# Two early product groups at each norm, a last norm without POOL, and a start with zero products: one decoder layer in fp32 on one core

## The chip, the core and the metric

The kernel runs on one core of a Trainium2 chip. The core has a matmul engine (PE, with a separate weight load, PEld), a vector engine (DVE), a scalar engine (ACT), a general engine (POOL) and an engine that issues the transfers (SP). Each runs its own instructions in order and waits on semaphores for the others. The metric is the device time of one execution in microseconds (us), as the median of several runs.

## The reference

One inference step of a decoder layer on 320 token columns: 256 of a new sequence and 8 x 8 of running ones. Weights and activations are fp32.

```python
x1 = layer_norm(ALPHA * x + 0.5 * swiglu_ffn(x, ffn1_w1, ffn1_w3, ffn1_w2), ln1_g, ln1_b)
proj = x1 @ w_in
q, k, v, o, ig, fg, glu_a, glu_b, gate_a, gate_b = jnp.split(proj, SPLIT_IDX, axis=-1)
h_a, (C_new, n_new, m_new) = mlstm_branch(q, k, v, o, ig, fg, ...)
h_b, conv_new = conv_branch(glu_a, glu_b, conv_buf, conv_w, conv_b, conv_ln_g, conv_ln_b)
mix = (sigmoid(gate_a) * h_a + sigmoid(gate_b) * h_b) @ w_out
x2 = layer_norm(ALPHA * x1 + mix, ln2_g, ln2_b)
y = layer_norm(ALPHA * x2 + 0.5 * swiglu_ffn(x2, ffn2_w1, ffn2_w3, ffn2_w2), ln3_g, ln3_b)
```

D_MODEL is 2048, D_FF 5632, there are four mLSTM heads, and the depthwise convolution has 31 taps. The results are y for both groups, the new mLSTM states and the new convolution caches.

## The kernel before

Activations lie transposed: 16 tiles of 128 features x 320 tokens. A product of a weight column (128 output features) is a sum over 16 tiles, one 128x128 weight block each. For fp32 accuracy each weight block and each activation tile is split into a high and a low part: ACT copies the high part (`whi`, L148; `xh`), DVE subtracts to get the low part (`wlo`, L149; `xl`). `mm3` issues three products per block: `xh`*`whi` (L213), `xl`*`whi` (L214), `xh`*`wlo` (L215).

`Stream` brings the weights in the order of use, in chunks of 512 KB (8 blocks), and splits them half a chunk at a time, three halves ahead. Accumulators are PSUM tiles: five named `acc`, three named `sm`.

The stages follow each other: FFN1, norm ln1, the mixer (products with w_in, the heads, the convolutions, the convolution's norm), the products with w_out, norm ln2, FFN2, the last norm ln3, output yT.

A norm needs the sums over all 16 tiles before its factor `r` is known (`Norm.finish`, then `rsqrt`, L239 to L243). Then each tile is scaled (`z`, L1094), and split with its bias (`affine_split`: `xh` on ACT at L500, `xl` on DVE at L501). So that PE has work in that time, `Norm.early` holds tiles `eh`, `el` of the tile that is centred but not yet scaled (`ahead`), with two columns more for the gain and the bias. `first_group` multiplies a first group of four weight columns with them; `normed` (L287 to L291, tile `late`) puts the factor and the offset into these results afterwards. At ln1 the group is the first two pairs of convolution inputs (`a`, `g`), at ln2 two pairs of FFN2's up-products.

Smaller work runs beside the products. `gemm` calls `tick` every four blocks, and a tick takes one step of each of four lanes: heads and gates in lane 0, norm steps in lane 1, two convolutions in lanes 2 and 3. `w_in_schedule` sets the order of the 112 columns of w_in: `a`/`g` pairs of the convolutions, one at each step, with the other columns spread over the steps; a head starts when its last `v` column is done (`head`, whose first product is `pb`, L674), and 16 `gb` columns and the last head's `o`/`ga` columns come at the end. In that end part the convolution's norm (`conv_out`, `th` at L248) and the last head's own norm (`mean` at L270 and `sq`) run.

The tile framework's scheduler decides from its own plan in which order each engine's instructions stand; `issue_after` keeps an instruction behind another one. All transfers are issued by SP and go through one queue.

Of the kernel before, what the change touches and what calls it, by code (L numbers as in the profile page):

```python
# [9 lines left out]
F32 = mybir.dt.float32  # L10
F32R = mybir.dt.float32r
AF = mybir.ActivationFunctionType
ALU = mybir.AluOpType
# [31 lines left out]
def w_in_schedule():  # L45


    def qkv(h):
        return ([("q", 2 * h + j) for j in range(2)] + [("k", 2 * h + j) for j in range(2)]
                + [("v", 4 * h + j) for j in range(4)])  # L50

    def oga(h):
        return [x for j in range(4) for x in (("o", 4 * h + j), ("ga", 4 * h + j))]

    others = qkv(0) + qkv(1) + oga(0) + qkv(2) + oga(1) + qkv(3) + oga(2)
    groups = [[("a", 0), ("g", 0), ("a", 1), ("g", 1)]]
    steps = range(2, KD)
    done = 0
    for n, i in enumerate(steps):
        groups += [[("a", i)], [("g", i)]]  # L60
        upto = len(others) * (n + 1) // len(steps)
        groups += [[x] for x in others[done:upto]]
        done = upto
    tail = [("gb", j) for j in range(KD)] + oga(3)
    return groups + [[x] for x in tail]
# [105 lines left out]
class Kernel:  # L171
    TICK = 4

# [43 lines left out]
    def gemm(self, accs, xs):  # L217

        n = len(xs)
        for k, (xh, xl) in enumerate(xs):  # L220
# [73 lines left out]
    def first_group(self, count, norm, name):  # L294

        accs = [self.acc(T + 2) for _ in range(count)]
        ys = []

        def tiles():
            for k in range(KD):  # L300
                ys.append(self.affine_split(*norm.scaled(k, name)))
                norm.z[k] = None
                yield

        self.later(tiles(), 1)
        self.gemm(accs, norm.early)
        self.drain((1,), lambda: len(ys) == KD)
        norm.early.clear()
        return [self.normed(ps, norm) for ps in accs], ys
# [9 lines left out]
    def build(self):  # L319
        tc, nc, a = self.tc, self.nc, self.a  # L320
        with (
# [10 lines left out]
            def x(n):  # L332
                k = len(xs)
                n = min(n, KD - k)
                raw = mp.tile([P, n * T], F32, tag="c0", name="xraw", bufs=3)
                nc.sync.dma_start(out=raw, in_=a["xT"][:, k * T:(k + n) * T])
                xs.extend(self.split(raw[:, i * T:(i + 1) * T]) for i in range(n))

            x(1)
# [81 lines left out]
    def ffn(self, n, xs, norm=None):  # L421
# [5 lines left out]
        for kind, q, ms in ffn_schedule():  # L427
            if kind == "up":
                if xs is None:
                    accs, xs = self.first_group(2 * len(ms), norm, "ln2")  # L430
# [28 lines left out]
    def last_norm(self, norm):  # L459

        nc = self.nc
        by_pe, by_pool = (0, 4, 8, 12), (3, 7, 11, 15)
        z, d = norm.z, {}

        def centre(k):
            eng = nc.gpsimd if k in by_pool else nc.vector
            eng.tensor_tensor(out=z[k], in0=z[k], in1=norm.mean, op=ALU.subtract)
            d[k] = z[k]

        with self.tc.issue_after(norm.sums.ins):  # L470
            for k in by_pe:
# [3 lines left out]
        for k in (3, 7, 1):  # L475
            centre(k)
        with self.tc.issue_after(norm.var.ins):
            for k in (2, 5, 6, 9, 11, 15):
                centre(k)
        first = None  # L480
        for k in list(d) + [k for k in range(KD) if k not in d]:
            with self.tc.issue_after((norm.last if k in d else first).ins):
                if k not in d:
                    centre(k)
                eng = nc.gpsimd if k in by_pool else nc.vector
                mul = eng.tensor_tensor(out=z[k], in0=d[k], in1=norm.r, op=ALU.mult)  # L486
                if eng is nc.vector and first is None:
                    first = mul
                g, b = self.scol("ln3_g", -0.5, k), self.col("ln3_b", k)
                if k % 3 == 1:  # L490
                    nc.vector.tensor_scalar(z[k], z[k], g, b, op0=ALU.mult, op1=ALU.add)
                else:
                    nc.scalar.activation(z[k], z[k], AF.Identity, scale=g, bias=b)
                nc.sync.dma_start(out=self.a["yT"][k], in_=z[k])
# [109 lines left out]
    def conv(self, i, acc_a, acc_g, done):  # L604
# [5 lines left out]
        nc.sync.dma_start(out=us[:, :, :HIST], in_=a["cache"][i])  # L610
# [273 lines left out]
    def mixer(self, before):  # L884
# [32 lines left out]
        self.silu_done = 0  # L917
        for n, group in enumerate(w_in_schedule()):
            if ys is None:
                accs, ys = self.first_group(len(group), before, "ln1")  # L920
# [35 lines left out]
            if n == 2:  # L956
                self.gates_product(ys)
# [221 lines left out]
```

## Time and profile before

| | |
|---|---|
| median of 3 runs | 2965.38 us (2963.70 to 2968.78) |
| profiled execution | 2962.41 us, its span 2960.6 us |
| instructions on PE | 19582 |
| mean granted PE clock | 0.993 |
| weights and other data read | 433.12 MB |

The span runs from the first to the last instruction of the profiled execution. Busy time is the time in which an engine worked; a busy PE can still be a slow one, since the granted clock may be half. A chunk of 8 blocks has 24 products. Line numbers in rows are those of the kernel before; in rows of the changed kernel the same lines stand a little lower (L213 becomes L214, L501 becomes L520).

### The profile page before, as it was taken

What the parts mean: (1) busy time and instruction counts of PE and PEld (TensorE: products, weight loads), DVE (VectorE), ACT (ScalarE), POOL (GpSimd) and SP (SyncE); (2) the same over time, 40 slices, a digit from 0 to 9 for tenths busy, and PEclk for the clock granted to TensorE, in tenths of its full rate; (3) what the DMA queues carried; (4) which work ended last, traced back from release to release, by engine and by line L of the source; (5) the groups of instructions that cost most, each with busy time, mean ns of one, the idle gap of its engine ahead of it and who ended that gap; (6) DMA issues with size and microseconds to landing.
All of it is one profiled execution on the core that took longest, in us unless ns stands there. A gap on an engine that the chain in (4) does not pass through costs nothing.

```text
span 2960.6 us, 50364 instructions
## 1 busy us (share of the span) xinstructions
PE 2900.5 (98%) x19582; PEld 2867.5 (97%) x19582; DVE 1892.2 (64%) x3491; ACT 1346.7 (45%) x2396; POOL 70.6 (2%) x76
## 2 busy tenths in 40 slices
PE   9999999999999899999999989999999999999997
PEld 9999999999999899999999979999999999999997
DVE  6544444444458999989989886578544444444447
ACT  5433433433445555555554555455433433433444
POOL 0100000000000000000000000200100000000001
PEclk9999999999999999999999999999999999999999
DMA  6444444444444456564565634444444444444443
GB/s 217 152 150 151 150 150 150 150 150 150 150 150 142 122 150 206 170 210 149 178 197 160 215 103 157 150 150 136 150 150 150 150 150 150 150 150 150 150 150 106
DMA packets 163264, 460.14 MB, mean 155 GB/s; under 512 B 50220, under 2 KB 53164, under 8 KB 163024
## 3 DMA queue, kind: packets, MB, share of 16 engines
q1 hardware_dynamic: 163024, 456.92, 47.4%
q8 instruction: 153, 2.51, 0.4%
q14 instruction: 87, 0.71, 0.1%
HBM read 433.12 MB, written 23.74 MB: 154 GB/s over the span
## 4 chain that ended last, share of the span: by engine, by line
PE 93%; DMA 2%; DVE 2%; ACT 1%; issue 0%; DVEq 0%; SPq 0%; ACTq 0%
PE acc L213 30%; PE acc L214 30%; PE acc L215 30%; DMA c<-in_C 1%; DMA out_C_s<-c 1%; PE ip L820 1%; DVE wlo L149 0%; PE cps L826 0%; PE sp L689 0%; ACT whi L148 0%; PE num L847 0%; DMA xraw<-in_xT 0%; DVE z L1094 0%; DVE z L486 0%; DVE c L827 0%
## 5 line engine op out<-in xcount | busy, mean ns | idle before, releaser
L149 DVE TENSOR_TENSOR wlo<-wraw,whi 128x512 fp32r<-128x512 f32 x1568 | 1086.7, 695 | 909.7 <-ACT whi L148 902.0
L148 ACT ACTIVATE whi<-wraw 128x512 fp32r<-128x512 f32 x1568 | 986.6, 631 | 1393.0 <-PE acc L214 1282.5
L213 PE MATMUL acc<-xh,whi 128*128 128x320 f32 x4480 | 1386.4, 311 | 24.0 <-ACT th L248 7.6
L214 PE MATMUL acc<-xl,whi 128*128 128x320 f32 x4480 | 1383.8, 309 | 6.9 <-DVE xl L501 6.9
L215 PE MATMUL acc<-xh,wlo 128*128 128x320 f32 x4480 | 1384.9, 310 | 0.7 <-DVE wlo L149 0.7
L213 PEld LDWEIGHTS acc<-xh,whi 128*128 128x128 f32 x4480 | 843.8, 189 | 31.8 <-ACT th L248 8.5
L214 PEld LDWEIGHTS acc<-xl,whi 128*128 128x128 f32 x4480 | 845.1, 189 | 12.1 <-DVE xl L501 8.0
L215 PEld LDWEIGHTS acc<-xh,wlo 128*128 128x128 f32 x4480 | 843.3, 188 | 5.7 <-DVE wlo L149 0.9
L214 PE MATMUL acc<-hl,whi 128*128 128x320 f32 x1408 | 433.9, 309 | 0.0
L213 PE MATMUL acc<-hh,whi 128*128 128x320 f32 x1408 | 432.9, 308 | 0.3 <-ACT whi L148 0.3
L215 PE MATMUL acc<-hh,wlo 128*128 128x320 f32 x1408 | 432.4, 309 | 0.0
L213 PEld LDWEIGHTS acc<-hh,whi 128*128 128x128 f32 x1408 | 264.3, 188 | 0.6 <-ACT whi L148 0.6
L214 PEld LDWEIGHTS acc<-hl,whi 128*128 128x128 f32 x1408 | 264.1, 188 | 0.0
L215 PEld LDWEIGHTS acc<-hh,wlo 128*128 128x128 f32 x1408 | 264.0, 188 | 0.0
L622 DVE SCALAR_TENSOR_TENSOR cy<-pu,cw,cy 128x256 f32<-128x256 f32 x480 | 222.6, 482 | 1.0
L448 DVE SCALAR_TENSOR_TENSOR z<-acc,z 128x320 f32<-128x320 f32 x128 | 62.8, 491 | 53.9 <-PE acc L215 52.3
L214 PE MATMUL acc<-ml,whi 128*128 128x320 f32 x256 | 79.1, 309 | 0.0
L213 PE MATMUL acc<-mh,whi 128*128 128x320 f32 x256 | 79.1, 309 | 0.0
L215 PE MATMUL acc<-mh,wlo 128*128 128x320 f32 x256 | 78.7, 309 | 0.0
L438 DVE TENSOR_TENSOR h<-s,acc 128x320 f32<-128x320 f32 x86 | 42.0, 488 | 53.3 <-ACT s L436 53.2
L315 POOL TENSOR_TENSOR z<-xh,xl 128x320 f32<-128x320 f32 x48 | 60.6, 1271 | 619.5 <-DVE h L438 353.6
L436 ACT ACTIVATE s<-acc 128x320 f32<-128x320 f32 x86 | 37.7, 438 | 70.2 <-PE acc L215 70.2
(289 smaller groups left out, 1661.9 us busy)
## 6 DMA issues: line engine op xcount, KB each, us to landing
wraw<-in_wst SPq DMA_DIRECT2D x783, 512.0 KB, 3.3
c<-in_C SPq DMA_DIRECT2D x32, 512.0 KB, 4.3
out_C_s<-c SPq DMA_DIRECT2D x32, 512.0 KB, 4.4
out_yT<-z SPq DMA_DIRECT2D x16, 160.0 KB, 1.8
out_C_p<-cn SPq DMA_DIRECT2D x4, 512.0 KB, 2.6
us<-in_cache SPq DMA_DIRECT2D x16, 120.0 KB, 4.5
out_conv_s<-us SPq DMA_DIRECT2D x16, 120.0 KB, 6.2
xraw<-in_xT SPq DMA_DIRECT2D x3, 480.0 KB, 4.4
```

Of the source, the lines that this page charges most:

```text
L148: nc.scalar.activation(hi, raw, AF.Copy)
L149: nc.vector.tensor_tensor(out=lo, in0=raw, in1=hi.bitcast(F32), op=ALU.subtract)
L213: mm(ps, hi, xh, start=first, stop=False)
L214: mm(ps, hi, xl, start=False, stop=False)
L215: mm(ps, lo, xh, start=False, stop=last)
L315: self.nc.gpsimd.tensor_tensor(out=t, in0=hi.bitcast(F32), in1=lo.bitcast(F32), op=ALU.add)
L436: nc.scalar.activation(s, accs[2 * j], AF.Silu)
L438: nc.vector.tensor_tensor(out=hh, in0=s, in1=accs[2 * j + 1], op=ALU.mult)
L448: nc.vector.scalar_tensor_tensor(out=z[m], in0=ps, scalar=0.5 / ALPHA, in1=z[m], op0=ALU.mult, op1=ALU.add)
L622: nc.vector.scalar_tensor_tensor(out=yp, in0=pu[:, w:w + SEQ], scalar=self.cw[:, i, w:w + 1], in1=yp, op0=ALU.mult, op1=ALU.add)
L820: mm(ip[:32, :], qc[j][:, bs], x, start=j == 0 and n == 0, stop=j == 1 and n == 1)
```

## The change

1. `first_group` becomes `first_groups`, a generator: the first group of four columns as before, then a second group of two columns (one `acc` and one `sm` accumulator) from the same early tiles, which are let go one by one (`clear`). The scaling steps are spread over more ticks. At ln1 the third `a`/`g` pair is moved into the second group; `steps` then has 13 entries instead of 14, over which the other 56 columns are spread. At ln2 the second group is FFN2's third pair. The gates' product is called after the second group.
2. `warm_up` sets a tile to zero and multiplies it 13 times by itself, ahead of all weights.
3. `consts` (and the first cache loads of the convolutions) are issued behind the last load of x.
4. `last_norm`: nine tiles instead of four are centred by PE (identity times tile, minus the mean), the other seven by DVE, none by POOL; all 16 gains and biases are applied by ACT, and the tiles go out in the order of their numbers.

```diff
-    groups = [[("a", 0), ("g", 0), ("a", 1), ("g", 1)]]
-    steps = range(2, KD)
+    groups = [[("a", 0), ("g", 0), ("a", 1), ("g", 1)], [("a", 2), ("g", 2)]]
+    steps = range(3, KD)
...
-    def first_group(self, count, norm, name):
-
-        accs = [self.acc(T + 2) for _ in range(count)]
+    def first_groups(self, norm, name):
+
         ys = []
 
         def tiles():
+            yield
+            yield
             for k in range(KD):
                 ys.append(self.affine_split(*norm.scaled(k, name)))
                 norm.z[k] = None
                 yield
-
+                if k % 3 == 2:
+                    yield
+
+        accs = [self.acc(T + 2) for _ in range(4)]
         self.later(tiles(), 1)
         self.gemm(accs, norm.early)
+        yield [self.normed(ps, norm) for ps in accs]
+        del accs
+        accs = [self.acc(T + 2), self.sm([P, T + 2], "acc")]
+        self.gemm(accs, norm.early, True)
         self.drain((1,), lambda: len(ys) == KD)
         norm.early.clear()
-        return [self.normed(ps, norm) for ps in accs], ys
+        yield [self.normed(ps, norm) for ps in accs]
+        yield ys
...
+            self.warm_up()
             x(1)
             for _ in st.load(CB // PB):
                 x(1)
...
-            self.consts(cp)
-            norm = self.ffn(1, xs)
+            norm = self.ffn(1, xs, cp=cp)
...
+    def warm_up(self):
+
+        x = self.t("zero", F32R)
+        self.nc.vector.memset(x.bitcast(F32), 0.0)
+        ps = self.sm([P, T], "zero")
+        for i in range(self.WARM):
+            self.nc.tensor.matmul(ps, x[:, :P], x, start=i == 0, stop=i == self.WARM - 1)
...
+            if i == 3 and cp:
+                with self.tc.issue_after(self.last_x):
+                    self.consts(cp)
...
-        by_pe, by_pool = (0, 4, 8, 12), (3, 7, 11, 15)
+        by_pe = (0, 1, 2, 4, 6, 8, 10, 12, 14)
+        by_dve = [k for k in range(KD) if k not in by_pe]
...
-        with self.tc.issue_after(norm.sums.ins):
-            for k in by_pe:
+        with self.tc.issue_after(norm.var.ins):
+            for k in by_dve[:3]:
+                centre(k)
+        prev = norm.last
+        for k in range(KD):
+            if k in by_pe:
                 d[k] = self.acc()
                 nc.tensor.matmul(d[k], self.ident, z[k], start=True, stop=False)
                 nc.tensor.matmul(d[k], self.minus_mean, norm.s, start=False, stop=True)
...
+            with self.tc.issue_after(prev.ins):
                 if k not in d:
                     centre(k)
...
+                prev = nc.vector.tensor_tensor(out=z[k], in0=d[k], in1=norm.r, op=ALU.mult)
+            nc.scalar.activation(z[k], z[k], AF.Identity, scale=self.scol("ln3_g", -0.5, k), bias=self.col("ln3_b", k))
+            nc.sync.dma_start(out=self.a["yT"][k], in_=z[k])
...
-            if n == 2:
+            if n == 1:
                 self.gates_product(ys)
```

What that does to the order shows at three places. A row is a line of the kernel, the operation and its tiles; x3 means three in a row.

SP at the start of the program, before: the constants `cst`, `btri`, `par` and `cw` stand between the loads of x.

```order
L136 DMA wraw<-in_wst 128x1024 x3
L356 DMA cst<-in_cst 128x360
L364 DMA btri<-in_cst 64x64
L336 DMA xraw<-in_xT 128x640
L368 DMA par<-in_par 128x160
L370 DMA cw<-in_cw 128x496
L336 DMA xraw<-in_xT 128x640
```

The same place in the changed kernel.

```order
L136 DMA wraw<-in_wst 128x1024 x3
L349 DMA xraw<-in_xT 128x640 x2
L136 DMA wraw<-in_wst 128x1024
L349 DMA xraw<-in_xT 128x960
L136 DMA wraw<-in_wst 128x1024 x3
L349 DMA xraw<-in_xT 128x960 x2
L377 DMA cst<-in_cst 128x360
```

The x loads have moved ahead of the constants, and directly behind the third chunk of weights.

DVE at ln1, before, from the norm's factor `r` on: all scaling (`z`) first, then all `xl`, then `late`, then the first convolution (`pu`, `us`).

```order
L243 SCALAR_TENSOR_TENSOR r<-rsq,r 128x320
L1088 TENSOR_TENSOR mr<-mean,r 128x320
L1094 SCALAR_TENSOR_TENSOR z<-z,ln_g_scaled,r 128x320 x15
L501 SCALAR_TENSOR_TENSOR xl<-z,par,xh 128x320
L1094 SCALAR_TENSOR_TENSOR z<-z,ln_g_scaled,r 128x320
L501 SCALAR_TENSOR_TENSOR xl<-z,par,xh 128x320 x15
L289 TENSOR_TENSOR late<-acc,r 128x320 x4
```

The same engine in the changed kernel, a later piece of the same stage, behind the first eleven `xl` and all `late` (`taps` and the reduction into `cy` are a convolution's sample tokens, `cy<-pu,cw,cy` is one tap).

```order
L663 TENSOR_REDUCE cy<-taps 128x32
L149 TENSOR_TENSOR wlo<-wraw,whi 128x512
L642 SCALAR_TENSOR_TENSOR cy<-pu,cw,cy 128x256
L633 TENSOR_TENSOR pu<-th,late 128x256
L634 TENSOR_TENSOR us<-th,late 128x8x8
L149 TENSOR_TENSOR wlo<-wraw,whi 128x512
L642 SCALAR_TENSOR_TENSOR cy<-pu,cw,cy 128x256
L661 TENSOR_TENSOR taps<-us,cw 128x992
L642 SCALAR_TENSOR_TENSOR cy<-pu,cw,cy 128x256
L520 SCALAR_TENSOR_TENSOR xl<-z,par,xh 128x320
```

The last row is the twelfth `xl`: the starts of two convolutions (`pu`, `us`, `taps`) and seven of their taps have moved ahead of or between the last five `xl`, and weight splits `wlo` stand among them.

PE at the last norm, before: the two sums, then the centring of four tiles (`cst` holds the identity).

```order
L1078 MATMUL ps<-ns,mean_d 128x320
L1079 MATMUL pq<-sq,mean_d 128x320
L473 MATMUL acc<-z,cst 128x320
L474 MATMUL acc<-ns,minus_mean 128x320
L473 MATMUL acc<-z,cst 128x320
```

PE at the last norm in the changed kernel.

```order
L506 MATMUL acc<-z,cst 128x320 x5
L1101 MATMUL ps<-ns,mean_d 128x320
L507 MATMUL acc<-ns,minus_mean 128x320 x5
L1102 MATMUL pq<-sq,mean_d 128x320
L506 MATMUL acc<-z,cst 128x320
L507 MATMUL acc<-ns,minus_mean 128x320
```

Five identity products have moved ahead of the first sum and five mean products ahead of the second.

More of the change, by code (lines that the diff above doesn't have):

```diff
@@ L172 @@
     TICK = 4
+    WARM = 13
     def __init__(self, tc, a):
@@ L215, in mm3, with gemm @@
         mm(ps, lo, xh, start=False, stop=last)
-    def gemm(self, accs, xs):
+    def gemm(self, accs, xs, clear=False):
         n = len(xs)
-        for k, (xh, xl) in enumerate(xs):
+        for k in range(n):
+            xh, xl = xs[k]
+            if clear:
+                xs[k] = None
             for ps in accs:
@@ L335, in x @@
                 raw = mp.tile([P, n * T], F32, tag="c0", name="xraw", bufs=3)
-                nc.sync.dma_start(out=raw, in_=a["xT"][:, k * T:(k + n) * T])
+                self.last_x = nc.sync.dma_start(out=raw, in_=a["xT"][:, k * T:(k + n) * T]).ins
                 xs.extend(self.split(raw[:, i * T:(i + 1) * T]) for i in range(n))
+            self.warm_up()
             x(1)
@@ L419, in consts, with ffn @@
             self.kst.append(t)
-    def ffn(self, n, xs, norm=None):
+    def ffn(self, n, xs, norm=None, cp=None):
         nc = self.nc
@@ L426, in ffn @@
         new = Norm(self, z, EPS / ALPHA ** 2, "ln1" if n == 1 else None, KD)
-        for kind, q, ms in ffn_schedule():
+        first = None if xs else self.first_groups(norm, "ln2")
+        for i, (kind, q, ms) in enumerate(ffn_schedule()):
+            if i == 3 and cp:
+                with self.tc.issue_after(self.last_x):
+                    self.consts(cp)
             if kind == "up":
-                if xs is None:
-                    accs, xs = self.first_group(2 * len(ms), norm, "ln2")
+                if first and i < 2:
+                    accs = next(first)
+                    if i == 1:
+                        xs = next(first)
                 else:
@@ L461, in last_norm @@
         nc = self.nc
-        by_pe, by_pool = (0, 4, 8, 12), (3, 7, 11, 15)
+        by_pe = (0, 1, 2, 4, 6, 8, 10, 12, 14)
+        by_dve = [k for k in range(KD) if k not in by_pe]
         z, d = norm.z, {}
         def centre(k):
-            eng = nc.gpsimd if k in by_pool else nc.vector
-            eng.tensor_tensor(out=z[k], in0=z[k], in1=norm.mean, op=ALU.subtract)
             d[k] = z[k]
-        with self.tc.issue_after(norm.sums.ins):
-            for k in by_pe:
+            return nc.vector.tensor_tensor(out=z[k], in0=z[k], in1=norm.mean, op=ALU.subtract)
+        with self.tc.issue_after(norm.var.ins):
[4 more added lines that the diff above has]
+            if k in by_pe:
                 d[k] = self.acc()
@@ L474, in last_norm @@
                 nc.tensor.matmul(d[k], self.minus_mean, norm.s, start=False, stop=True)
[L475 to L482, printed above, removed]
+            with self.tc.issue_after(prev.ins):
                 if k not in d:
                     centre(k)
[L485 to L494, printed above, removed]
+                prev = nc.vector.tensor_tensor(out=z[k], in0=d[k], in1=norm.r, op=ALU.mult)
+            nc.scalar.activation(z[k], z[k], AF.Identity, scale=self.scol("ln3_g", -0.5, k), bias=self.col("ln3_b", k))
+            nc.sync.dma_start(out=self.a["yT"][k], in_=z[k])
     def affine_split(self, u, b):
@@ L609, in conv @@
         us = mp.tile([P, NB, SEGW], F32, tag="us", name="us", bufs=2)
-        nc.sync.dma_start(out=us[:, :, :HIST], in_=a["cache"][i])
+        with self.tc.issue_after(self.last_x):
+            nc.sync.dma_start(out=us[:, :, :HIST], in_=a["cache"][i])
         sg = self.sigmoid(acc_g)
@@ L917, in mixer @@
         self.silu_done = 0
+        first = self.first_groups(before, "ln1")
         for n, group in enumerate(w_in_schedule()):
-            if ys is None:
-                accs, ys = self.first_group(len(group), before, "ln1")
+            if n < 2:
+                accs = next(first)
+                if n == 1:
+                    ys = next(first)
             else:
@@ L955, in mixer @@
                     mixed(i)
-            if n == 2:
+            if n == 1:
                 self.gates_product(ys)
```

## The prediction

> **What bounds the kernel now.** I read the page first (busy time), then the list of what PE waited for, then windows around those waits, and last the timeline at each place. In a timeline row the first number is microseconds from the start of the span, the second the time that the printed group covers.
>
> ```profile
> PE 2900.5 (98%) x19582; PEld 2867.5 (97%) x19582; DVE 1892.2 (64%) x3491; ACT 1346.7 (45%) x2396; POOL 70.6 (2%) x76
> ```
> The matmul engine PE is the bound: 60 us of the span are not its own. The change removes no weight product, so it can only win back places where PE stands or runs slowly. The waits (total, times, longest):
>
> ```profile
> PE acc L213 <- ACT th L248: 7.6, 3, 4.1
> PE acc L214 <- DVE xl L501: 6.9, 4, 5.9
> PE acc L213 <- ACT xh L500: 2.9, 1, 2.9
> PE pb L674 <- DVE parts L599: 1.4, 1, 1.4
> ```
> The rows of xl and xh L500 are the norms ln1 and ln2; th and pb are the mixer (a wait for late and one for mean follow below, where they lie). Windows around them (length; busy us and count of PE, PEld, DVE, ACT, POOL; then the granted PE clock) show that a wait also costs clock:
>
> ```profile
> 967.00:985.00 18.00, 9.22 (x45) 8.57 (x44) 17.77 (x42) 9.62 (x20) 0.00 (x0) 0.72 0.16 52
> 1030.00:1060.00 30.00, 27.66 (x174) 26.49 (x173) 28.79 (x87) 16.16 (x31) 0.12 (x1) 0.94 0.42 141
> 1700.00:1800.00 100.00, 85.53 (x568) 83.52 (x567) 83.20 (x173) 58.41 (x116) 0.00 (x0) 0.93 0.38 126
> 2030.00:2050.00 20.00, 15.93 (x90) 14.40 (x89) 17.67 (x41) 12.89 (x27) 0.00 (x0) 0.91 0.26 90
> ```
> The pace without waits is in the first two rows of the last fence: 19 steps from 2935.69 to 2938.48, 0.147 us a product. So ln1 lost 18 - 45 x 0.147 = 11.4 us and ln2 lost 20 - 90 x 0.147 = 6.8 us. These two are what the second group is set against.
>
> **The change, part by part.** *Start: zero products, x ahead of the constants.*
>
> ```profile
> 4.83 1.43 PE L213 MATMUL acc<-xh,whi 128*128 128x320 f32 x4 [4.83 <-ACT whi L148]
> 8.20 1.27 PE L213 MATMUL acc<-xh,whi 128*128 128x320 f32 x4
> 13.68 0.85 PE L213 MATMUL acc<-xh,whi 128*128 128x320 f32 x4 [1.12 <-ACT xh L263]
> 13.16 0.47 ACT L263 ACTIVATE xh<-xraw 128x320 fp32r<-128x320 f32 x1 [0.64 <-DMA xraw<-in_xT]
> 9.08 1.15 ACT L148 ACTIVATE whi<-wraw 128x512 fp32r<-128x512 f32 x2 [2.27 <-DMA wraw<-in_wst]
> 10.45 1.16 ACT L148 ACTIVATE whi<-wraw 128x512 fp32r<-128x512 f32 x2 [0.21 <-DMA wraw<-in_wst]
> ```
> The first twelve products took 3.37 us (4.83 to 8.20), 0.281 each, nearly twice the pace. Thirteen zero products at that price are 3.65 us, and fit into the 4.83 us in which PE waits. If they raise the clock, the first 24 real products finish some 2.3 us sooner. But that is given back twice: the third tile's products need the weights whose split starts at 9.08, and the fourth tile's need the x that landed at 13.14. What sets the end of the start is that x. In the new order it stands directly behind the weights, without cst (184 KB) and btri ahead of it; 184 KB at the rate of the 512 KB chunks (two are split 1.4 us apart as they land, at 9.08 and 10.45) are 0.5 us. I take a gain of 0.5 us for the whole start; ends: +1.7 us (PE now waits in two pieces before 13 us, and the clock falls for one period) and -2.5 us (all the cold pace). The constants and the cache loads that move behind the last x are first used where the first norm begins, hundreds of us later, and cost nothing: the whole of FFN1 hides them.
>
> *ln1.*
>
> ```profile
> 970.79 0.41 PE L213 MATMUL acc<-xh,whi 128*128 128x320 f32 x1 [2.85 <-ACT xh L500]
> 977.13 0.63 PE L214 MATMUL acc<-xl,whi 128*128 128x320 f32 x1 [5.93 <-DVE xl L501]
> 968.66 0.49 DVE L243 SCALAR_TENSOR_TENSOR r<-rsq,r 128x320 f32<-128x320 f32 x1
> 969.59 7.02 DVE L1094 SCALAR_TENSOR_TENSOR z<-z,ln_g_scaled,r 128x320 f32<-128x320 f32 x15
> 977.45 7.02 DVE L501 SCALAR_TENSOR_TENSOR xl<-z,par,xh 128x320 fp32r<-128x320 f32 x15
> 985.99 1.29 DVE L149 TENSOR_TENSOR wlo<-wraw,whi 128x512 fp32r<-128x512 f32 x2
> 992.61 0.42 DVE L613 TENSOR_TENSOR pu<-th,late 128x256 f32<-128x256 f32 x1 [1.68 <-ACT th L253]
> 993.75 1.19 DVE L641 TENSOR_TENSOR taps<-us,cw 128x992 f32<-128x992 f32 x1
> 995.85 1.18 DVE L643 TENSOR_REDUCE cy<-taps 128x32 f32<-128x992 f32 x1
> ```
> Before, PE stops at 967.9 (970.79 less 2.85). Now it has 96 more products (two columns of 16 tiles, three each) that need no r: 14.1 us, to 982.0. That covers both old waits. Then DVE must be there in time. Along its new order, from r at 968.66 to the last xl, I add: r, mr and six small copies 1.3; 16 z and 16 xl at 0.47, 15.0; thirteen wlo at 0.61, 7.9; eight steps of late at 0.4 to 0.47, 3.5; two conv starts (pu with us 0.5, which is 992.61 to 993.75 less one wlo; taps 1.1, reduce 1.1), 5.4; seven taps of cy at 0.40, 2.8. Both conv starts stand ahead of the last five xl in the new order. That is 35.9 us, to 1004.6. PE's rows up to the one that needs the last xl (137 products: 32 of the gates, the rest of three columns) take it to 982.0 + 20.1 = 1002.1. So PE loses 2.5 us behind DVE, plus the 1.7 us that DVE itself waits for th (row of 992.61, now ahead of xl), plus half a clock period, 1.7 us (3.4 us at half pace, as ln2 had). Loss 5.9, gain 11.4 - 5.9 = 5.5 us; ends 0 (DVE waits for ACT at each conv start as well) and 9.
>
> *Clock.* In ln2 a wait of 0.7 and one of 2.4 us were enough for a clock of 0.91 over 20 us, that is 20 x 0.09 x 2 = 3.6 us at half rate.
> [...]
>
> *Mixer, middle.* The gates start one place earlier in the schedule and the heads complete two columns (32 blocks, 14.1 us) later. So at pb the parts are ready: 1.4 us of wait, the half clock after it (0.06 x 30 x 2 = 3.6 us at half pace, 1.8 us) and some slow products behind it go, 3.9 us in all. Ends 0 and 6: the other small waits there are moved, not removed.
>
> *Mixer, end.*
>
> ```profile
> 1750.58 0.63 PE L270 MATMUL mean<-xh,one 128*128 128x320 f32 x1 [5.47 <-ACT xh L263]
> 1755.89 0.64 PE L213 MATMUL acc<-xh,whi 128*128 128x320 f32 x1 [4.11 <-ACT th L248]
> 1768.62 0.41 PE L213 MATMUL acc<-xh,whi 128*128 128x320 f32 x1 [2.98 <-ACT th L248]
> ```
> 12.6 us of waits, where the conv norm and the last head's norm meet on ACT and DVE; with some clock (0.93 over 100 us is 14 us at half rate, most of it spent waiting) about 13.9. The convs end 8 blocks earlier, the last head 32 blocks later. Following ACT and DVE along the new order from the conv norm's sums, I find three waits again (0.8, 4.9 and 3.0 us, at the first th, behind the head's squares, and behind the table loads of the head's root) and 1.7 us of clock: 10.4. Gain 3.5; ends -4 (a loss) and 10, since this is a sum over about a hundred rows of two engines.
>
> *ln2.*
>
> ```profile
> 2041.00 0.60 PE L213 MATMUL acc<-xh,whi 128*128 128x320 f32 x1 [2.41 <-DVE late L289]
> 2040.36 1.70 DVE L289 TENSOR_TENSOR late<-acc,r 128x320 f32<-128x320 f32 x4
> ```
> late waited in DVE's queue behind 16 xl. The second group gives DVE 14.1 us while no conv stands in its way, and late now comes ahead of the last xl. I leave 1.3 to 1.8 us for single waits on xl and wlo: gain 5 us of 6.8; ends 2 and 6.8.
>
> *Last norm.*
>
> ```profile
> 2935.69 0.31 PE L214 MATMUL acc<-hl,whi 128*128 128x320 f32 x1
> ...
> 2938.48 0.31 PE L215 MATMUL acc<-hh,wlo 128*128 128x320 f32 x1
> 2940.54 0.70 PE L1079 MATMUL pq<-sq,mean_d 128*128 128x320 f32 x2
> 2941.08 0.70 PE L473 MATMUL acc<-z,cst 128*128 128x320 f32 x2
> 2941.61 0.70 PE L474 MATMUL acc<-ns,minus_mean 128*128 128x320 f32 x2
> 2941.75 4.71 DVE L467 TENSOR_TENSOR z<-z,mean 128x320 f32<-128x320 f32 x5
> 2946.90 0.49 DVE L243 SCALAR_TENSOR_TENSOR r<-rsq,r 128x320 f32<-128x320 f32 x1
> 2952.42 1.28 DVE L467 TENSOR_TENSOR z<-z,mean 128x320 f32<-128x320 f32 x3
> 2951.73 3.38 ACT L493 ACTIVATE z<-z,par,ln_g_scaled 128x320 f32<-128x320 f32 x6 [0.41 <-DVE z L486]
> 2956.41 0.65 ACT L493 ACTIVATE z<-z,par,ln_g_scaled 128x320 f32<-128x320 f32 x1 [1.30 <-DVE z L486]
> ```
> Beside POOL five centres took 4.71 us on DVE, alone three took 1.28. Those five stood between the sums and r; now three do, without POOL: about 3 us less. But in the new order five identity products (0.54 each, 2941.08 to 2941.61) stand ahead of the sum ps and five mean products ahead of pq: pq starts at 2938.63 + 11 x 0.535 = 2944.5 instead of 2940.54, 4.0 us more. From pq's start to r without a queue are 3.9 us (pq 0.7, then v, three ACT steps and two DVE steps at about L243's 0.49, and hand-overs), so r ends at 2948.4, against 2947.4. Then ACT is the bound: 16 affines at 3.38 / 6 = 0.56 us after a first product of some 0.5: 2957.9, against 2957.1 before; and the last centred tiles wait for PE at half clock, up to 1.2 us. I take 1.5 us of loss; ends +3 and -4 (the new products run while PE would wait for ns anyway).
>
> *Sum:* -0.5 - 5.5 - 3.9 - 3.5 - 5.0 + 1.5 = -16.9 us against the profiled execution of 2962.41 us (span 2960.6), so 2945.5. That execution lies 3.0 us below the median of the runs, 2965.38; against the median the same sum gives 2948.5, and I predict 2948.
>
> **The rivals.** *DVE is the bound behind ln1.* Its queue is full there (17.77 of 18 us from 967 on), and the conv starts stand ahead of the last xl. If each conv start also waits for ACT, ln1 and the middle of the mixer give nothing: -16.9 + 9.4 = -7.5, 2958. For it speaks DVE's 28.79 of 30 us at 1030; against it that PE may run two columns up to the eleventh xl.
> *All parts reach their good ends in the norms and in the tail:* another 3.5 at ln1, 1.8 at ln2 and 5.5 in the last norm: 2937.
> *Cancelled:* the mixer only reshuffles (0 instead of -7.4) and the end of the mixer is worse by 4: -5.5, 2960; with the tail at +3 too, 2962. So the change would not do what it is built to do.
> *Slower:* the last head's chain runs 14.1 us later with the same columns behind it. If it has no slack, the whole 14.1 us become wait, on top of the old 13.9, and PE goes through it at half clock (10 us at half pace, 5 us): 19 us instead of a gain of 3.5, sum +5.6, 2971. It decides from 33 us of waits at the end of the mixer on; against it speaks that only part of what PE waited for there was the head.
>
> **How the numbers follow.** Forecast 0.47, DVE the bound 0.18, good ends 0.12, cancelled 0.15, slower 0.08. The first three are faster by over 0.2% (5.9 us, about what a measurement of this kernel can tell from no change): 0.77; same 0.15; slower 0.08. The range 2938 to 2964 leaves out the slower case, half of the good ends and a little of the cancelled one.
>
> **What would show it.** Right: no wait for xh at 968, a clock of 1.00 to 982, then one to three waits for xl or wlo between 985 and 1005; no pb wait; ln2 with under 2 us of waits; five identity products right behind the last weight product, and r about 10 us after it; the first real product at the full pace, but the fourth tile still near 13 us. Wrong: a wait over 6 us near 995, more than 14 us of waits where the conv norm meets the last head, or a start that ends before 11 us.

## The result and the profile after

| | before | after |
|---|---|---|
| median | 2964.54 us (4 runs, 2963.36 to 2968.78) | 2985.22 us (4 runs, 2983.35 to 2987.57) |
| ratio | | 1.0065, 95% interval 1.0052 to 1.0078 |
| span of the profiled execution | 2960.6 us | 2982.5 us |
| mean granted PE clock | 0.993 | 0.987 |

The change makes the kernel 0.65% slower; forecast were 2948 us and a range of 2938 to 2964. The page of the changed kernel, its busy line and the shares of the chain that ended last:

```profile
PE 2927.7 (98%) x19615; PEld 2890.0 (97%) x19615; DVE 1893.1 (63%) x3502; ACT 1350.5 (45%) x2405; POOL 61.5 (2%) x68
...
PE acc L214 30%; PE acc L216 30%; PE acc L215 30%; DMA c<-in_C 2%; DMA out_C_s<-c 2%; DVE cy L642 1%; PE ip L840 0%; DVE wlo L149 0%; PE num L867 0%; DVE c L847 0%; ACT chi L826 0%; PE acc L531 0%; DMA xraw<-in_xT 0%; PE acc L506 0%; ACT whi L148 0%
```

PE is busy 27 us longer with almost the same instructions, so it ran slowly somewhere; and the loads and stores of the mLSTM states (`c`) have a larger share of the chain, 1.6% and 1.5% instead of 1.1% and 1.0%. The list of what PE waited for (total, times, longest):

```profile
PE acc L214 <- ACT th L252: 13.4, 4, 4.3
PE ip L840 <- ACT chi L826: 8.1, 4, 4.0
PE acc L216 <- DVE wlo L149: 7.2, 2, 5.9
PE acc L531 <- DVE late L293: 4.5, 1, 4.5
...
PE c L274 <- ACT xh L267: 3.5, 1, 3.5
```

The waits for `xl` and `xh` of the norms are gone, as meant. What has grown is `ip`, the products of a head's loop over its eight running states: 8.1 us behind `chi`, where before had 1.9.

To see where the time went I take, in each trace, the start of the n-th of the 18816 weight products (`mm3` with `whi` or `wlo`). From it I take off the time that PE's other products (heads, sums, gates) before it need at full pace, since the two kernels have done different numbers of those by then; the pace of each kind is the lower quartile of its steps to the next product. What is left moves only by waits and by slow products. Its difference to before, in us:

| weight product | where | at, in before | after minus before |
|---|---|---|---|
| 6500 | start and FFN1, before ln1 | 963.6 | -1.7 |
| 6700 | behind ln1 | 1010.3 | -6.9 |
| 7000 | behind the gates' rows | 1063.1 | +0.3 |
| 8000 | behind head 0 | 1240.6 | +3.1 |
| 9000 | behind head 1 | 1423.6 | +28.9 |
| 10500 | ahead of the mixer's end | 1678.9 | +30.2 |
| 11200 | behind it | 1814.0 | +25.5 |
| 12600 | before ln2 ends | 2020.3 | +25.7 |
| 12800 | behind ln2 | 2056.8 | +18.8 |
| 18800 | end of FFN2 | 2936.3 | +20.9 |
| (end of the span) | last norm | 2960.6 | +21.8 |

Both norms gain, ln1 5.2 us and ln2 6.8 us, and the mixer's end 4.7. The mixer's first half takes all of it and more: 7.2 us at the gates' rows and 25.8 us from 8000 to 9000, at head 1. Windows of the changed kernel (length; busy us and count of PE, PEld, DVE, ACT, POOL; granted clock, share of the DMA engines, GB/s) show the same places:

```profile
967.00:985.00 18.00, 13.53 (x91) 13.26 (x90) 17.97 (x40) 10.05 (x19) 0.00 (x0) 0.93 0.35 116
...
1036.00:1054.00 18.00, 10.85 (x52) 10.18 (x51) 17.94 (x56) 6.18 (x13) 0.12 (x1) 0.72 0.17 57
...
1350.00:1360.00 10.00, 2.82 (x7) 0.80 (x7) 6.44 (x13) 2.45 (x5) 0.00 (x0) 0.73 0.73 238
1360.00:1370.00 10.00, 6.01 (x21) 4.52 (x22) 7.50 (x16) 2.64 (x5) 0.25 (x2) 0.50 0.51 157
1370.00:1380.00 10.00, 9.47 (x40) 9.01 (x40) 6.51 (x16) 3.03 (x8) 0.00 (x0) 0.50 0.00 0
...
1340.00:1395.00 55.00, 39.64 (x190) 33.87 (x189) 43.10 (x89) 21.28 (x43) 0.25 (x2) 0.73 0.46 137
...
2030.00:2055.00 25.00, 25.00 (x171) 25.00 (x169) 24.92 (x60) 15.07 (x31) 0.00 (x0) 1.00 0.39 122
```

and of before over the same time, all of it at full clock (its head 1 is through by 1341):

```profile
1340.00:1395.00 55.00, 52.15 (x351) 50.87 (x351) 51.72 (x114) 31.97 (x63) 0.00 (x0) 1.00 0.44 129
```

161 products fewer in 55 us, at 0.147 us a product, are 23.7 us. The timeline of PE in the changed kernel (start, us, engine, line, operation, out<-in; in brackets the idle time ahead and what ended it):

```profile
1348.87 0.62 PE L846 MATMUL cps<-vst,kst 128*128 128x512 f32 x2
1353.46 0.42 PE L840 MATMUL ip<-chi,cat 128*32 128x512 f32 x1 [3.97 <-ACT chi L826]
...
1359.36 0.63 PE L840 MATMUL ip<-chi,cat 128*32 128x512 f32 x1 [3.13 <-ACT chi L826]
...
1366.49 0.63 PE L274 MATMUL c<-xh,one 128*128 128x320 f32 x1 [3.51 <-ACT xh L267]
...
1376.43 0.63 PE L214 MATMUL acc<-xh,whi 128*128 128x320 f32 x1
...
1381.66 0.39 PE L215 MATMUL acc<-xl,whi 128*128 128x320 f32 x1
```

Between 1348.0 and 1376.4 there is no weight product at all: 28.4 us in which PE has only 17 products of head 1's last states (`ip`, `cps`), two of a sum and the head's 39 `num`. Before, the longest such stretch at this head was 8.6 us (from 1328.5), with 6 products of states and the same 39 `num`. The head's loop over the states now begins at 1309.6 instead of 1279.4, 30.2 us later, while the next head's first `q` column ends only 2.2 us later (1313.7, before 1311.5). A state goes round load, `chi` on ACT, `ip`, update on DVE, store, in some 5.7 us, which weight products hid before and nothing hides now. ACT in the same stretch:

```profile
1352.78 1.15 ACT L826 ACTIVATE chi<-c 128x512 fp32r<-128x512 f32 x2 [3.12 <-DMA c<-in_C]
1358.67 1.15 ACT L826 ACTIVATE chi<-c 128x512 fp32r<-128x512 f32 x2 [4.74 <-DMA c<-in_C]
...
1364.19 1.15 ACT L826 ACTIVATE chi<-c 128x512 fp32r<-128x512 f32 x2 [3.76 <-DMA c<-in_C]
...
1372.98 0.44 ACT L1051 ACTIVATE nc<-c 128x320 f32<-128x320 f32 x1 [6.54 <-PE c L274]
...
1375.96 0.42 ACT L950 ACTIVATE q<-acc 128x320 f32<-128x320 f32 x1
```

The first three rows wait for a state's load. The last is the copy that empties an accumulator (the first `q` column of head 2), behind all of these in ACT's order; the first weight product follows it at once, at 1376.43. That is what PE was short of: a column of w_in is 48 weight products in one of the five accumulators, and five columns had ended by 1348.3 (`q`, `a`, `g`, `q`, `k`, the first at 1313.7), none of which was taken up before this copy, 62.3 us behind its column. Before, five columns had ended as well by 1328.8, but one of them was a `g` column whose `th` came ahead of the `q` copy (1339.54) in ACT's order, and the weight products went on at 1337.1:

```profile
1335.55 0.42 ACT L248 ACTIVATE th<-acc 128x320 f32<-128x320 f32 x1
```

The idle times ahead of PE from 1348 to 1391 sum to 15.4 us (3.97, 0.57, 3.13, 0.50, 3.51, 0.53, 0.25, 2.92). From 1354.5 to 1381.8 the products also run at half clock: 27.3 us less 8.2 of those waits, half of it lost, are 9.5. Together 24.9. Counted over all weight products from 8000 to 9000, PE waits 17.8 us (before 4.5) and is at half clock for 34.1 us, 8.6 of them waits (before none): 13.3 and 12.8 us more than before, 26.1 where the table has 25.8.

The second place, at the gates' rows:

```profile
1034.46 1.28 ACT L612 ACT_TABLE_LOAD   x1
1046.69 0.26 ACT L612 ACTIVATE rows<-rows 4x64 f32<-4x64 f32 x1 [10.95 <-DVE rows L611]
1046.05 0.64 PE L216 MATMUL acc<-xh,wlo 128*128 128x320 f32 x1 [5.87 <-DVE wlo L149]
```

ACT has loaded the table for an exponential and stands for 10.95 us behind DVE's rows of the gates; the splits of the weights (`whi`, then `wlo`) stand behind it, and PE runs out of weights.

### The profile page after: what moved, and what is told of

Its sections match the earlier page's. It is cut to its first block, busy times and chain, and to the rows that moved or that the text cites. A ratio compares the mean times of both kernels' runs of the same rounds, so it can differ in the third digit from the quotient of the medians.

```text
span 2982.5 us, 50458 instructions
## 1 busy us (share of the span) xinstructions
PE 2927.7 (98%) x19615; PEld 2890.0 (97%) x19615; DVE 1893.1 (63%) x3502; ACT 1350.5 (45%) x2405; POOL 61.5 (2%) x68
## 4 chain that ended last, share of the span: by engine, by line
PE 92%; DMA 3%; DVE 2%; ACT 1%; issue 1%; ACTq 0%; DVEq 0%
PE acc L214 30%; PE acc L216 30%; PE acc L215 30%; DMA c<-in_C 2%; DMA out_C_s<-c 2%; DVE cy L642 1%; PE ip L840 0%; DVE wlo L149 0%; PE num L867 0%; DVE c L847 0%; ACT chi L826 0%; PE acc L531 0%; DMA xraw<-in_xT 0%; PE acc L506 0%; ACT whi L148 0%
## 5 line engine op out<-in xcount | busy, mean ns | idle before, releaser
L214 PE MATMUL acc<-xh,whi 128*128 128x320 f32 x4416 | 1372.2, 312 | 15.6 <-ACT th L252 13.4
L215 PE MATMUL acc<-xl,whi 128*128 128x320 f32 x4416 | 1369.2, 310 | 0.0
L215 PEld LDWEIGHTS acc<-xl,whi 128*128 128x128 f32 x4416 | 836.7, 190 | 3.9
```

The lines of the kernel that those rows point to most:

```text
L214: mm(ps, hi, xh, start=first, stop=False)
L215: mm(ps, hi, xl, start=False, stop=False)
```

## The experiments

The theory was that the loss is made by the order of the columns of w_in alone (13 steps instead of 14: PE is left without weight products while a head works), not by the second groups, the start or the last norm. Rivals: the first group's results, which hold accumulators at ln1; the last norm; the mixer as such, whatever one does to its order. Each run is compared with before on the same chip.

**The changed kernel with the columns in before's order** (the second group keeps the third pair).

```diff
-    steps = range(3, KD)
+    steps = range(2, KD)
...
-        groups += [[("a", i)], [("g", i)]]
+        if n:
+            groups += [[("a", i)], [("g", i)]]
```

> The changed kernel with the w_in columns in the order of the kernel before: the third a/g pair stays in the second group, then four other columns, then the steps as before, so each head is complete at the same column as before. Theory 1 (the column order: heads complete two columns later while the later columns keep their places, so head 1's loop over the eight states runs into the copy of head 2's first q and PE is left with bare state products around 1350 us): the stall of some 30 us goes, 2955 us (2948 to 2962). Theory 2 (the second group itself, its accumulators and its load on DVE, costs the mixer the time): it stays above 2978.

Measured: 2968.63 us, ratio 0.9999 (0.9984 to 1.0014). The loss is gone, the gain isn't there; the time lies between the two expectations. Counted as in the table, it is 9.9 us ahead of before at 7000, 3.6 ahead at 8000, and 7.0 behind at 9000: head 1 again has a stretch without weight products, 19.6 us long, in its timeline with these waits:

```profile
1329.14 0.42 PE L841 MATMUL ip<-chi,cat 128*32 128x512 f32 x1 [2.54 <-ACT chi L827]
1336.59 0.64 PE L841 MATMUL ip<-chi,cat 128*32 128x512 f32 x1 [5.09 <-ACT chi L827]
```

So before's order of columns is better by some 17 us, but what is gained ahead of the heads is still lost at head 1.

**Before with the new order of columns, and nothing else.**

```diff
-    steps = range(2, KD)
+    groups += [[("a", 2)], [("g", 2)]]
+    steps = range(3, KD)
```

> The kernel before with the new column order alone (the third a/g pair as two single columns behind the first group, the other 56 columns over 13 steps), one early group at each norm. Theory 1: slower, 2980 to 2992 us, with a stall of state products near 1350 us. Theory 2: 2960 to 2969 us.

Measured: 2987.47 us, ratio 1.0064 (1.0044 to 1.0085), as much as the change loses in all, by the schedule alone. The losses lie at the same two places: 9.2 us between products 6700 and 7000 and 9.7 between 8000 and 9000, with 5.0 more up to 10000; 16.4 us without weight products at head 1. Its window there:

```profile
1340.00:1395.00 55.00, 48.99 (x268) 44.94 (x267) 49.19 (x98) 24.81 (x49) 0.25 (x2) 0.81 0.54 165
```

**Before with the new last norm** (its `last_norm` replaced by that of the change).

```diff
-        by_pe, by_pool = (0, 4, 8, 12), (3, 7, 11, 15)
+        by_pe = (0, 1, 2, 4, 6, 8, 10, 12, 14)
+        by_dve = [k for k in range(KD) if k not in by_pe]
...
```

> The kernel before with the new last norm alone. By the tail of the changed kernel's trace (23.1 us from the last weight product to the end, 22.2 before) it costs 0.9 us: 2965.5 us, the same within the measurement. Rival: the ten products ahead of pq cost their whole 4 us: 2968.5.

Measured: 2965.69 us, ratio 0.9997 (0.9986 to 1.0007), and 22.1 us from the last weight product to the end, as before (22.2). Taking POOL out of the last norm neither costs nor brings anything.

**The changed kernel without its part at ln1** (before's first group, columns and place of the gates; start, ln2 and last norm kept).

```diff
-    groups = [[("a", 0), ("g", 0), ("a", 1), ("g", 1)], [("a", 2), ("g", 2)]]
-    steps = range(3, KD)
+    groups = [[("a", 0), ("g", 0), ("a", 1), ("g", 1)]]
+    steps = range(2, KD)
...
-            if n == 1:
+            if n == 2:
```

> The changed kernel with the first norm and the w_in columns as before; kept are the start, the second group at ln2 and the last norm. If these parts are worth what their places in the trace show (start -0.8, ln2 -6.8, tail +0.9): 2957.8 us. If the loss also comes from them, or moves the mixer by itself: 2966 or more.

Measured: 2969.29 us, ratio 1.0008 (0.9997 to 1.0019): the sum of the parts misses, and the second expectation came. ln2's 6.8 us are there, but from 8000 to 9000 11.8 us are lost: PE waits 3.4 and 1.6 us for `chi`, 1.2 for `st` and 3.9 for head 1's mean. The mixer's program is that of before, columns and all, but its instructions stand in another order: between 1000 and 1800 us of the traces the sequences of operations differ in 82 places on PE, 227 on DVE and 91 on ACT (the kernel with the new last norm alone has before's sequence there). So the order of columns isn't the only thing that uncovers head 1; the scheduler moves the work around it with an edit elsewhere. Which of the three parts that this kernel keeps does it was not tried.

**The changed kernel with buffers of their own for the `q` tiles of the later heads.** All small tiles share one pool, and in the built program their first writes stand on each engine in the order in which the program asks for them, so a `q` copy can't go ahead of the head's work on ACT.

```diff
-                    t = self.t(x)
+                    t = self.tp.tile([P, T], F32, tag="q", name="q", bufs=2) if x == "q" and i >= 4 else self.t(x)
...
-        pt = mp.tile([P, 448], F32, tag="pt", name="pt", bufs=1)
+        pt = dt
```

(The second edit makes room for the buffers.)

> The changed kernel with two buffers of their own for the q tiles of heads 2 and 3 (taken out of the pool of 72 that all small tiles share; one scratch tile of the head is reused in place to make room). Theory 1a (the copy of head 2's first q waits in order behind head 1's results hv, because both come from the one shared pool, so its accumulator stays taken and PE has only bare state products from the fifth column on): the stall from 1340 to 1390 us shrinks by 15 to 25 us, 2960 to 2970 us. Theory 1b (the state loop itself takes longer, by its transfers of C, whatever PE may do beside it): no change, 2980 or more.

Measured: 2972.16 us, ratio 1.0019 (1.0010 to 1.0029): 13 us of the loss are gone, at a time just above the 2960 to 2970 that were expected. The copy of head 2's first `q` now comes 0.5 us behind its column (at 1314.4) instead of 62.3. The stretch without weight products at head 1 begins 19 us later and is 19.4 us long instead of 28.4, and no state is in it; what is left are 52 `num`, two products each of a sum and a mean, and among them waits of 0.9, 0.9, 3.5 and 2.6 us. The window beside that of the changed kernel (39.64 us busy, clock 0.73):

```profile
1340.00:1395.00 55.00, 46.20 (x272) 42.75 (x271) 50.38 (x101) 25.07 (x51) 0.25 (x2) 0.84 0.55 165
```

So the accumulator that waits for its copy is a cause. What is left has the same form: at 1367.2 the five columns that have ended are `a`, `g`, two `k` and a `v`, whose copies still go through the shared pool, and PE goes on when `th` has taken up the first of them:

```profile
1386.56 0.64 PE L214 MATMUL acc<-xh,whi 128*128 128x320 f32 x1 [2.60 <-ACT th L252]
```

How much of the 13 us is the buffers' own and how much the plan that moves with any edit (the kernel above shifted 12 us at this head) was not separated.

**Before's columns, and the first group's results taken up only behind the second group,** the gates' product in one of the small accumulators.

```diff
-        yield [self.normed(ps, norm) for ps in accs]
-        del accs
-        accs = [self.acc(T + 2), self.sm([P, T + 2], "acc")]
-        self.gemm(accs, norm.early, True)
+        two = [self.acc(T + 2), self.sm([P, T + 2], "acc")]
+        self.gemm(two, norm.early, True)
         self.drain((1,), lambda: len(ys) == KD)
         norm.early.clear()
         yield [self.normed(ps, norm) for ps in accs]
+        del accs
+        yield [self.normed(ps, norm) for ps in two]
...
-        g8 = self.acc()[:4 * H, :]
+        g8 = self.sm([P, T], "acc")[:4 * H, :]
```

> e1 (changed kernel, old column order) with the results of the first early group taken up only after the second group, so that all xl stand ahead of the first two convolutions, and with the gates' product in a small accumulator. Theory 3 (the gates and heads are a chain of their own from ln1 to about 1345 us, PE's gain at ln1 is lost where it meets that chain, and in e1 the chain starts 9 us later because the gates' product waits for late and for the last xl): gates' product ends by 995 instead of 1007.8, head 1's loop starts 6 us or more sooner than e1's 1288, 2953 to 2960 us. Theory 4 (the loss of 13 us at 1240 to 1340 us in e1 is C's transfers or chance of the plan): gates sooner, but the total within 4 us of e1 (2965 to 2970).

Measured: 2964.89 us, ratio 0.9996 (0.9986 to 1.0007). At ln1 it does what it should; PE's wait for `late` is gone, and the window reads 17.20 us busy instead of 13.53:

```profile
967.00:985.00 18.00, 17.20 (x113) 14.85 (x111) 17.97 (x38) 12.32 (x24) 0.00 (x0) 1.00 0.37 115
```

It is 13.4 us ahead of before at 7000 and 12.5 at 7500, then 2.0 ahead at 8000 and 8.4 behind at 9000. The gain at ln1 is real and is lost again where PE meets the heads. The gates' product ends at 988.2 instead of the 1007.8 of the first experiment, and head 1's loop begins 12.6 us sooner, both as the first expectation had it; the total, 3.7 us below that experiment's, is what the second one had. So a late start of the gates and heads isn't all that takes the gain.

**That kernel with the `q` buffers, and with the sums ahead of the centring products in the last norm.**

```diff
+                with self.tc.issue_after(norm.sums.ins):
-                nc.tensor.matmul(d[k], self.ident, z[k], start=True, stop=False)
-                nc.tensor.matmul(d[k], self.minus_mean, norm.s, start=False, stop=True)
+                    nc.tensor.matmul(d[k], self.ident, z[k], start=True, stop=False)
+                    nc.tensor.matmul(d[k], self.minus_mean, norm.s, start=False, stop=True)
```

> e6 with the q buffers of e5, and with the sums of the last norm ahead of the centring products on PE. The tail from the last weight product to the end falls from 23.1 to about 19 to 20 us (r is 4 us sooner). By theories 1a and 3 together 2945 to 2955 us; if theory 4 holds, the tail alone, about 2962.

Measured: 2954.86 us (2952.77 to 2959.30), ratio 0.9961 (0.9948 to 0.9974): faster than both kernels. Head 1's stretch is 3.8 us long. Of the 10.7 us of span against the run above, 6.8 are gained up to the mixer's end (from 8000 to 9000 it loses 2.1 us instead of 10.4), and 3.9 in the last norm, whose timeline now begins with the sums:

```profile
2934.37 0.31 PE L217 MATMUL acc<-hh,wlo 128*128 128x320 f32 x1
2935.79 0.81 PE L1103 MATMUL ps<-ns,mean_d 128*128 128x320 f32 x2 [1.11 <-DVE ns L1027]
2936.43 0.73 PE L1104 MATMUL pq<-sq,mean_d 128*128 128x320 f32 x2
...
2939.88 0.49 DVE L248 SCALAR_TENSOR_TENSOR r<-rsq,r 128x320 f32<-128x320 f32 x1
...
2941.01 8.83 ACT L514 ACTIVATE z<-z,par,ln_g_scaled 128x320 f32<-128x320 f32 x16 [1.68 <-DVE z L513]
```

`r` comes 5.5 us behind the last weight product, and ACT's 16 steps follow without a gap: 18.1 us from that product to the end. The lead of ln1 is still not kept: it is 11.1 us at 7700, 1.4 at 8000 and gone at 9000 (0.7 behind). So this kernel's gain is ln2 and the last norm. Most of the lead goes at one wait of head 0 and the half clock with it (0.83 over the window from 1200 to 1230, which is 10.2 us at half rate, a part of them in the wait):

```profile
1219.28 0.64 PE L275 MATMUL var<-xh,one 128*128 128x320 f32 x1 [6.54 <-ACT xh L268]
```

**The same with the columns of heads 2 and 3 earlier.**

```diff
-    others = qkv(0) + qkv(1) + oga(0) + qkv(2) + oga(1) + qkv(3) + oga(2)
+    others = qkv(0) + qkv(1) + qkv(2) + oga(0) + qkv(3) + oga(1) + oga(2)
```

> The best kernel so far (e7) with one change in the order of the mixer's columns: head 2's q, k, v come before head 0's o and gate columns, and head 3's before head 1's, so that these two heads start and end earlier and head 3's chain is over before the convolution's norm. Nothing is added or removed. Theory 1 (PE is tied to the head chains through its five accumulators, so what counts is that no two chains meet): e7 still had 4.5 us and 6.85 us of waits at heads 0 and 1 and its convolution norm meets head 3 with some 14 us of waits and half clock; moving head 3 away saves most of that: span 2930 to 2945, time about 2938, with the whole gain between 1500 and 1800 us of the span. Rival (waits there are set by the convolution's norm itself on ACT and DVE, whatever the head does): 2950 to 2958, no difference between 1700 and 1800 us.

Measured: 2973.78 us, ratio 1.0018 (1.0005 to 1.0032). Both expectations miss. 12.7 us ahead of before at 8000, it is 15.6 behind at 9000 and 32.4 at 10500, then 23.5 at 11000. Its waits:

```profile
PE acc L215 <- ACT th L253: 17.5, 5, 9.7
PE ip L842 <- ACT chi L828: 10.9, 3, 5.1
```

The end of the mixer does what the theory said: from 10500 to 11000 it gains 8.9 us on before, the run above 1.4, so the rival fails there. But heads 1 and 2, whose columns now come one after the other, lose 28.3 us (8000 to 9000) and 16.1 (to 9500), with `ip` waiting 10.9 us in all. The theory named that sort of loss and did not look for it at these heads.

**The changed kernel with one zero product.**

```diff
-    WARM = 13
+    WARM = 1
```

> The changed kernel with 1 zero product in place of 13; the later constants stay. Only the first 61 weight products are compared, against before and after. If the later constants make the start's gain (the prediction's step): product 49 stands 0.5 to 0.8 us earlier than before, as in the changed kernel. Rival (the zero products make it, by a faster clock): product 49 stands within 0.2 us of before. In both the first twelve products run at the slow pace of 0.28 us each. The total should stay within 3 us of the changed kernel's 2985.

Measured, one profile: product 49 stands 0.39 us ahead of before, the changed kernel's 0.73 us, between the two expectations. Inconclusive: the other kernels with the same start as the changed one have that product between 1.35 us ahead and 0.09 behind, more than the half microsecond in question. Its first twelve weight products take 0.285 us each, as expected (before 0.281), and in the changed kernel 0.225: there the zero products count. The one time, 2980.53 us, lies 4.7 below the changed kernel's median.

## Why the prediction was wrong, point by point

**Start: right in size.** Gain 0.7 us, forecast 0.5, both within what profiles of one start differ by. The zero products do shorten the first weight products, but not all of them as foreseen: four still take 0.30 us each, the next eight 0.19, so the first twelve end 0.6 us sooner (by 7.58 instead of 8.20):

```profile
1.25 3.83 PE L372 MATMUL zero<-zero 128*128 128x320 f32 x13 [1.25 <-DVE zero L369]
4.88 1.40 PE L214 MATMUL acc<-xh,whi 128*128 128x320 f32 x4
6.08 0.83 PE L215 MATMUL acc<-xl,whi 128*128 128x320 f32 x4
...
7.58 0.86 PE L214 MATMUL acc<-xh,whi 128*128 128x320 f32 x4
...
12.94 0.86 PE L214 MATMUL acc<-xh,whi 128*128 128x320 f32 x4 [1.19 <-ACT xh L267]
```

The fourth tile's `x` sets the end, at 12.94 instead of 13.68, as the prediction had it. The granted clock reads 1.00 up to 15 us in both traces, so the slow first products don't show in it, and neither does the rise or the fall that the prediction reckoned with.

**ln1: the gain was right (5.2 us, forecast 5.5), its price another one.** PE waited for no `xh` or `xl`; the last `xl` ended at 1004.95, where the prediction had 1004.6. PE waited once, 4.52 us, for an accumulator that the first group still held:

```profile
984.40 1.69 DVE L293 TENSOR_TENSOR late<-acc,r 128x320 f32<-128x320 f32 x4
985.04 0.43 PE L531 MATMUL acc<-xh,wgp 128*16 128x320 f32 x1 [4.52 <-DVE late L293]
```

The four `late`, which free these accumulators, stand behind the `xl` in DVE's order. The prediction counted DVE's work and not what it frees; that both came to some 5 us is chance. The rival of DVE as the bound has a part of it: ln1's gain was given back by product 7000, at the gates' rows, where DVE is busy 17.94 of 18 us. Its price, no gain at these two places, is far from the loss that came, most of which lies at head 1.

**Mixer, middle: the step that failed.** It said: "The gates start one place earlier in the schedule and the heads complete two columns (32 blocks, 14.1 us) later. So at pb the parts are ready", a gain of 3.9 us with the ends 0 and 6. Measured from 6700 to 9000: a loss of 35.8 us. The wait at `pb` did go. But the gates' product, for all its earlier place, ended at 1007.5 instead of 998.4, and the step asked only what waits ahead of a head, not what covers the head behind. The heads came later and the columns behind them did not: head 1's columns were complete 12.9 us later (1191.5 instead of 1178.6), much as forecast, but its loop began 30.2 us later, while the next head's `q` column ended 2.2 us later. That column's copy stood behind the loop on ACT, the five accumulators were full, and the last three states of head 1 stood bare on PE for 28.4 us. That a head needs cover was in the list of waits of before:

```profile
PE ip L820 <- ACT st L821: 2.2, 2, 1.4
PE ip L820 <- ACT chi L806: 1.9, 2, 1.4
```

Such waits, small and several, said that this loop was only just hidden. And "moved, not removed" was given the end 0, as if a moved wait could not grow. At the gates, too, 7.2 us were lost, since ACT stood behind DVE's rows with the weights' splits behind it.

**The rival "slower" had the mechanism at the wrong place.** It foresaw a head's chain without columns behind it, with PE at half clock, 14.1 us of wait and 5 of clock, at the last head; it came at head 1, with 15.4 and 9.5. **The mixer's end itself: right in size**, a gain of 4.7 us, forecast 3.5. PE's waits from 1700 to 1825 fall from 14.5 to 9.2 us (forecast 8.7); the head's wait for its mean, 5.5 us, is gone, and two for `th` stay. The half clock there is 13.7 us in both.

**ln2: right.** Gain 6.8 us, forecast 5; the window of 2030 to 2055 has no wait and clock 1.00.

**Last norm: right in its steps.** From the last weight product to the end 23.1 us instead of 22.2, a loss of 0.9 against 1.5 forecast; but six other kernels with this same last norm have 22.0 to 22.1, so the norm itself costs nothing that shows. The steps hold: five pairs of products before and behind the sum, and `r` 9.5 us behind the last weight product where about 10 was said.

```profile
2959.40 0.31 PE L216 MATMUL acc<-hh,wlo 128*128 128x320 f32 x1
2959.55 2.85 PE L506 MATMUL acc<-z,cst 128*128 128x320 f32 x10
2962.24 0.70 PE L1101 MATMUL ps<-ns,mean_d 128*128 128x320 f32 x2
2962.77 2.86 PE L507 MATMUL acc<-ns,minus_mean 128*128 128x320 f32 x10
2965.47 0.70 PE L1102 MATMUL pq<-sq,mean_d 128*128 128x320 f32 x2
...
2968.89 0.49 DVE L247 SCALAR_TENSOR_TENSOR r<-rsq,r 128x320 f32<-128x320 f32 x1
```

**Not foreseen:** FFN2 takes 2.1 us more from 12800 to 18800. All kernels with a second group at ln2 show 1.1 to 2.9 us there, those without 0.0 and 0.1. Its cause stays open.

None of the three signs that were to show the prediction wrong appeared: 4.5 us was the longest wait near 995, 9.2 us the waits at the mixer's end, and the start ended at 12.94. They watch the norm, the start and the mixer's end; the loss came between, at head 1.

**Shown and not shown.** Shown: the net loss is that of the column order (21 us put into before, 17 us back when taken out of the change). It is not all that the mixer loses: of the 35.8 us from 6700 to 9000, about 14 stay with before's columns, and they use up what the norms gain. At head 1 PE runs out of accumulators, as the copies in the trace show, and own buffers for the `q` tiles give back 13 us. Not settled: which edit makes the kernel without its part at ln1 lose 12 us at head 1 with before's columns, and what exactly heads 1 and 2 lack when heads 2 and 3 come earlier. In all of these runs the loss is read as head products without weight products around them, but which edit causes it could be said only afterwards.

## What to carry to other kernels

When a change shifts the main stream of products against side chains that run beside it, count in the order of the main engine, for each chain, how long a stretch it has to itself, and compare that with the chain's time for one step: here the two orders differed by 28.4 against 8.6 us, and one could have read the count, 17 products of states instead of 6, before any run. The count warns and doesn't give the length: with before's columns in the change 18 such products took 19.6 us. A wait gained at one place becomes a gain in the total only if the next meeting with such a chain has slack; seven of these kernels, the change among them, were 6 to 10 us ahead of before at product 6700, behind ln1, and none was still ahead at 9000, behind head 1. An accumulator here was free only when its reader's engine had come to the copy, 62.3 us behind the column for head 2's first `q`, so the reader's order counts as much as its load: with five of them, see which of five columns in a row is taken up first, and when.

## What the runs showed of the hardware

In head 1's stretch of the changed kernel the granted clock fell to 0.50 at 1354.5, behind a wait of 3.97 us, and stayed there up to 1381.8, although PE was busy 9.47 of the 10 us from 1370 on. From the product that begins at 1366.49 it took 15.2 us to the first faster one, at 1381.66; the last 5.2 of them were the dense 320-column weight products from 1376.43 on. Before, at ln2, the clock fell at 2040.6, inside the wait of 2.41 us, and the weight products that begin at 2041.00 were at full pace 3.0 us later:

```profile
2043.54 0.47 PE L213 MATMUL acc<-xh,whi 128*128 128x320 f32 x1
2043.81 0.40 PE L214 MATMUL acc<-xl,whi 128*128 128x320 f32 x1
2044.04 0.31 PE L215 MATMUL acc<-xh,wlo 128*128 128x320 f32 x1
```

So the half clock lasted 3.4 us there, from which the prediction took its 1.7 us for ln1, and 27.3 us at head 1; the other such stretches of these two traces last from 3.4 to 13.7 us. At head 1 the short `num` products, of 32 to 256 columns, kept PE occupied from 1366.93 on, as far as the profile's busy time tells, and the clock under them stayed at 0.50. What brings it up again no run here shows. With this half clock the waits among these small products cost 1.6 times what the list of waits shows: 15.4 us of waits, 24.9 us in all.
